# A two-block transformer layer on one core: regrouped RWKV and attention products, token and adaptive-vector work moved ahead, and a priority for one stream

## The chip, the cores and the metric

The kernel is one program on one core of a Trainium2 chip. The time is microseconds of the device, from the first to the last instruction of the execution and what lies around it. TensorE (PE in the profile) multiplies, VectorE (DVE) and ScalarE (ACT) work on tiles element by element, GpSimd (POOL) computes a few powers, and SyncE (SP) issues nearly all transfers. Matmul results go to PSUM, everything else lives in SBUF or in device memory.

## What is computed

Two blocks follow each other on a sequence of 1024 tokens of width 1024, all in float32. The first mixes tokens by sliding-window attention and by an RWKV-7 recurrence, then comes a feed-forward with a three-tap convolution; the second modulates its input by adaptive vectors made from a condition `c`, and mixes by two gated linear attentions and a stick-breaking attention.

```python
def first_block(...):
        h = rms_norm(x, norm_mix_pre[l])
        proj = h @ w_in[l]
        q, k, v, p = jnp.split(proj, (D_ATTN, D_ATTN + D_KV, D_ATTN + 2 * D_KV), axis=-1)
        attn = sliding_window_sink_attention(q, k, v, rel_bias, sinks[l])
        ...
        rw = rwkv7_time_mix(p, ...)
        mix = jnp.concatenate([attn, rw.astype(x.dtype)], axis=-1) @ w_out[l]
        x = x + rms_norm(mix, norm_mix_post[l])
        f = conv_gated_ffn(rms_norm(x, norm_ffn_pre[l]), w_ffn_up[l], conv_w[l], conv_b[l], w_ffn_down[l])
        x = x + rms_norm(f, norm_ffn_post[l])

def second_block(...):
        ada = c_act @ w_ada[l] + b_ada[l]
        shift, scale, gate = jnp.split(ada, 3, axis=-1)
        h = rms_norm_2(x) * (1.0 + scale[:, None, :]) + shift[:, None, :]
        p = h @ w_in[l]
        ...
        y = jnp.concatenate([o_a, o_b, o_c], axis=-1) @ w_out[l]
        x = x + gate[:, None, :] * y
    return rms_norm_2(x) * final_norm_w
```

## The kernel before

**Products.** Every large product is made of three: both operands are split into a high and a low part (`hi`/`lo`, `wh`/`wl`, by `split`: ACT copies the high part, DVE subtracts it), and `gemm` (L151) adds high x low, low x high and high x high in PSUM. Weights arrive by `load_parts` (L135) in tiles of 256 KB, `wr`, three buffers deep. Inputs of a projection stand transposed, features on partitions: `to_h` (L232) transposes four 128 x 128 pieces on PE into a PSUM tile, ACT copies the high part, DVE makes the low part. Small products (RWKV, attention, gated linear attention) are plain float32; a float32 matmul leaves two records in the trace.

**Tokens.** They go in two halves of 512. Each half is projected (`proj1`), mixed, put through `w_out` (`out_rows`, L743 to L745), normalised (`post_mix`) and transposed into the feed-forward's input `h`.

**Streams.** Work is written as Python generators. `weave` takes the next step of the stream whose own clock is furthest behind, where each step yields a cost and a stream has a rate; a stream can also give its instructions a priority (`ahead`, which becomes `tc.high_priority(offset=...)`). A scheduler then puts the instructions of each engine in one fixed order, by these priorities and by its own estimate of when operands are ready. An engine runs its own list in order, so one that waits holds all behind it. Memory is by pools: a tile of a pool that is opened later can lie where tiles of a closed pool lay, and waits until they are free.

There are four such weaves around the change:

1. projection of both halves, `rwkv_a`, `rwkv_b`, `rwkv_c` of the first four pieces of 128 tokens, with attention beside (`attend`);
2. `enter` (the first half's `out_rows`, `post_mix` and `to_h`, two row tiles at a time) with the rest of attention, and `rest` (RWKV of the last four pieces) beside. Its priority is `AM`, and there is none. Behind it attention's pools are closed and the feed-forward's pool `fp` is opened in the room that they leave;
3. the feed-forward of both halves (`ffn`, units of `w_up` and `w_down`), with `between`: after the last RWKV piece (`("c", 7)`) it does the second half's `out_rows`, `post_mix` and `to_h`, then `ada_vectors`, then the second block's first projection;
4. `fill`, the second block's projections (`units`, in the order `ORD`) and `out_rows`, beside `gated` (gated linear attention) and `sticks` (stick-breaking).

**`rwkv_c`.** For each piece of 128 tokens and each chunk `c` of 64, with `j` over four pairs of heads and `h` over the two heads of a pair: L594 multiplies the running state `St` (rows 0 to 63 or 64 to 127, by head) into `ou[h][0:64, 1]`, DVE adds that to `UV`; L601 makes the state's increment; L606 (state) and L608 (inside the chunk) add up in `ou[h][.., 0]`, one right behind the other for each `j` and `h`. `ou[0]` and `ou[1]` are two banks of PSUM.

**Attention.** Blocks of 128 queries. Scores are made for four groups `w`, one PSUM buffer of the two of pool `psa` each (L664), DVE adds the bias and takes the maximum (L668), ACT takes the exponent, PE transposes (L686) into the same two buffers, ACT copies, PE multiplies by the values (L698) into a buffer that is held to the block's end, and L720 transposes the result.

**`ada_vectors`.** Three vectors of 1024. For each, eight row blocks of `w_ada` are loaded (512 KB, two buffers `wa`) and added up on DVE with the weight `sc[:, k]` into `m`; a product with ones sums over partitions (L950, in PSUM pool `psx`), the bias is added, and a row is written to device memory.

**`proj2(1)`.** After the last unit of the first half, it loads the second block's tokens 4 to 7, normalises (`pre2`), transposes each, and only then begins with units of the second half. `hi` and `lo` have one buffer, so the new input is written when the old one has been read for the last time.

```python
            for i in range(4):
                xs = new_xs()
                pre2(4 + i, xs, *w)
                to_h(xs, i, hi, lo)
                yield 3
```

## Time and profile before

| what | value |
|---|---|
| time, median of 3 runs | 2600.23 us (2585.8 to 2609.15) |
| time of the profiled execution | 2600.69 us |
| its span, first to last instruction | 2598.9 us |
| mean granted TensorE clock | 0.968 |
| busy share of PE, weight loads, DVE, ACT, POOL | 95%, 75%, 65%, 45%, 4% |
| DMA | 320.78 MB, mean 123 GB/s |

Busy times of engines are sums over the span. A row of a group gives line, engine, operation, tiles and shapes, count, busy time, mean of one, and the idle time of the engine ahead of it with what ended most of it. A row in order of time gives start, duration, engine, line, operation, tiles, shapes and how many instructions were merged, and in brackets the idle time ahead and what ended it. A row of a stretch gives its bounds, its length, busy time and instructions of PE, weight loads (PEld), DVE, ACT and POOL, the granted TensorE clock as a share of full speed, the share of DMA engines busy, and GB/s. Matmuls overlap, so the step from one start to the next is the price of one, not its duration.

### The profile page before, as it was taken

The numbers are of one execution on the slowest core, as the hardware profiler recorded it, in microseconds if no ns is written. First come the engines' busy times: TensorE is split into PE (matmuls) and PEld (weight loads), VectorE is DVE, ScalarE is ACT, GpSimd is POOL, SyncE is SP. The second block draws the span as 40 slices with busy tenths as digits, with TensorE's granted clock in tenths as the row PEclk, the third lists the DMA queues.
The fourth block names the chain that finished last, engine by engine and source line by source line (L and its number), as shares of the span: only waits on it lengthen the run. The fifth ranks groups of instructions, "written<-read, shape, count | busy, mean of one in ns | idle before, by whom it ended". The sixth has DMA issues, their size and how long they took to land.

```text
span 2598.9 us, 40965 instructions
## 1 busy us (share of the span) xinstructions
PE 2480.5 (95%) x15310; PEld 1940.4 (75%) x15310; DVE 1695.4 (65%) x3676; ACT 1171.0 (45%) x2205; POOL 99.4 (4%) x138
## 2 busy tenths in 40 slices
PE   7999999899999999999988999999999989999987
PEld 5777777678787787878776888778887766777665
DVE  5466653664675674755687655545567897878887
ACT  4344332463433533334443333443345665566864
POOL 1001000000000000000000000000000000000000
PEclk9999998889999999999999999999999989999988
DMA  6433223542232332324486432243346425342437
GB/s 205 145 111 102 69 77 100 159 128 81 86 97 72 94 94 69 96 70 130 136 278 199 130 98 94 83 130 121 94 139 208 132 97 159 123 129 77 143 132 251
DMA packets 219998, 320.78 MB, mean 123 GB/s; under 512 B 56956, under 2 KB 95508, under 8 KB 219799
## 3 DMA queue, kind: packets, MB, share of 16 engines
q1 hardware_dynamic: 219798, 318.17, 38.9%
q8 instruction: 120, 1.97, 0.3%
q14 instruction: 80, 0.65, 0.1%
HBM read 270.88 MB, written 47.21 MB: 122 GB/s over the span
## 4 chain that ended last, share of the span: by engine, by line
PE 73%; DVE 10%; issue 6%; DMA 4%; ACT 4%; POOL 2%; SPq 0%; POOLq 0%; DVEq 0%; ACTq 0%
PE g L151 37%; PE d L151 11%; PE gr L743 2%; DVE wl L78 1%; PE gr L744 1%; PE gr L745 1%; DMA wa<-in_w_ada_dram 1%; PE ou L608 1%; PE ou L606 1%; PE R L1463 1%; PE ra L495 1%; PE s L1359 1%; PE a_ps L698 1%; DMA wr<-in_w_out_dram 1%; PE x L743 1%
## 5 line engine op out<-in xcount | busy, mean ns | idle before, releaser
L75 ACT ACTIVATE wh<-wr 128x512 fp32r<-128x512 f32 x712 | 443.7, 626 | 664.3 <-PE g L151 223.2
L151 PE MATMUL g<-hi,wl 128*128 128x512 f32 (+1 forms) x1680 | 678.0, 404 | 7.9 <-DVE wl L78 3.4
L151 PE MATMUL g<-hi,wh 128*128 128x512 f32 (+1 forms) x1680 | 668.9, 398 | 0.0
L151 PE MATMUL g<-lo,wh 128*128 128x512 f32 (+1 forms) x1680 | 667.6, 397 | 0.0
L78 DVE TENSOR_TENSOR wl<-wr,wh 128x512 fp32r<-128x512 f32 x712 | 484.4, 684 | 224.9 <-ACT wh L75 223.1
L151 PEld LDWEIGHTS g<-hi,wl 128*128 128x128 f32 (+1 forms) x1680 | 317.6, 189 | 86.3 <-issue 6.3
L151 PEld LDWEIGHTS g<-hi,wh 128*128 128x128 f32 (+1 forms) x1680 | 317.5, 189 | 72.5 <-issue 3.1
L151 PEld LDWEIGHTS g<-lo,wh 128*128 128x128 f32 (+1 forms) x1680 | 317.8, 189 | 71.6 <-issue 5.1
L81 DVE SCALAR_TENSOR_TENSOR cv<-g,CW,cv 128x511 f32<-128x511 f32 (+1 forms) x256 | 190.5, 744 | 186.0 <-ACT cv L75 185.8
L151 PE MATMUL d<-hh,wl 128*128 128x512 f32 x512 | 204.1, 403 | 7.1 <-DVE wl L78 2.2
L151 PE MATMUL d<-hl,wh 128*128 128x512 f32 x512 | 202.8, 396 | 0.1
L151 PE MATMUL d<-hh,wh 128*128 128x512 f32 x512 | 201.9, 395 | 0.0
L75 ACT ACTIVATE cv<-g,CW 128x512 f32<-128x512 f32 x128 | 99.5, 777 | 195.3 <-PE g L151 195.1
L78 DVE TENSOR_TENSOR acc<-d,acc 128x512 f32<-128x512 f32 x112 | 76.5, 688 | 83.4 <-PE d L151 83.3
L151 PEld LDWEIGHTS d<-hh,wl 128*128 128x128 f32 x512 | 96.9, 190 | 34.3 <-DVE acc L78 4.4
L151 PEld LDWEIGHTS d<-hl,wh 128*128 128x128 f32 x512 | 97.2, 190 | 22.5 <-DVE hl L78 2.8
L151 PEld LDWEIGHTS d<-hh,wh 128*128 128x128 f32 x512 | 97.1, 190 | 20.2
L743 PE MATMUL gr<-wl,hi 128*128 128x512 f32 x200 | 84.7, 424 | 6.3 <-DVE wl L78 4.6
L744 PE MATMUL gr<-wh,lo 128*128 128x512 f32 x200 | 81.0, 405 | 1.7 <-DVE lo L78 1.7
L745 PE MATMUL gr<-wh,hi 128*128 128x512 f32 x200 | 80.4, 402 | 0.0
L125 POOL TENSOR_TENSOR rs<-ms,half_c 128x1 f32<-128x1 f32 x48 | 31.1, 650 | 1129.4 <-DVE ms L85 1118.7
L75 ACT ACTIVATE hh<-cv 128x512 fp32r<-128x512 f32 x64 | 40.4, 631 | 70.1 <-DVE cv L78 69.7
(484 smaller groups left out, 3634.0 us busy)
## 6 DMA issues: line engine op xcount, KB each, us to landing
wr<-in_w_up_dram SPq DMA_DIRECT2D x256, 256.0 KB, 2.7
wr<-in_w_in_dram SPq DMA_DIRECT2D x160, 256.0 KB, 2.8
wr<-in_w_down_dram SPq DMA_DIRECT2D x128, 256.0 KB, 2.7
wr<-in_w_out_dram SPq DMA_DIRECT2D x100, 256.0 KB, 2.9
wr<-in_w_values_dram SPq DMA_DIRECT2D x64, 256.0 KB, 2.8
xt<-x SPq DMA_DIRECT2D x24, 512.0 KB, 4.6
wa<-in_w_ada_dram SPq DMA_DIRECT2D x24, 512.0 KB, 4.7
xt<-in_x_dram SPq DMA_DIRECT2D x16, 512.0 KB, 3.7
```

What stands on the lines that cost most here:

```text
L75: S.activation(out=out, in_=in_, func=func, **kw)
L78: (eng or V).tensor_tensor(out=out, in0=in0, in1=in1, op=op)
L81: V.scalar_tensor_tensor(out=out, in0=in0, scalar=scalar, in1=in1, op0=op0, op1=op1)
L125: G.tensor_tensor(out=dst, in0=src, in1=half_c[0:src.shape[0], 0:src.shape[1]], op=ALU.pow)
L151: T.matmul(out=ps, lhsT=l, rhs=r, start=(first and n == 0), stop=(last and n == 3 * len(wk) - 1))
L495: T.matmul(out=gp[:, q, :], lhsT=flat(BK[hb:hb + 64, 4 * b + q, :, :]), rhs=flat(AR[hb:hb + 64, 4 * b + q, 0:2, :]), start=True, stop=True)
L606: T.matmul(out=ou[h][ob:ob + 64, 0, j, :], lhsT=AR[hb:hb + 64, 2 * j + c, 0, :], rhs=St[hb:hb + 64, j, :], start=True, stop=False)
L608: T.matmul(out=ou[h][ob:ob + 64, 0, j, :], lhsT=MT[:, 2 * j + c, h, 0:64], rhs=UV[:, 2 * j + c, hb:hb + 64], start=False, stop=True)
L698: T.matmul(out=pv[:, h, :], lhsT=pt[:, i, kb, :], rhs=vtok[:, n - 1 + kb, 64 * g:64 * g + 64], start=(kb == kbs[0]), stop=(kb == 1))
L743: T.matmul(out=p, lhsT=hi[:, k, tok], rhs=wl, start=first, stop=False)
L744: T.matmul(out=p, lhsT=lo[:, k, tok], rhs=wh, start=False, stop=False)
L745: T.matmul(out=p, lhsT=hi[:, k, tok], rhs=wh, start=False, stop=last)
```

## The change

Four things change, and no product is added or dropped.

In `rwkv_c`, L594's products take the heads in turn for each pair `j`, both additions to `UV` follow, all products of the state (L606) come next, then the increment, then all products inside the chunk (L608). The first of the state's products of a bank clears it, the others add.

In `attention`, two groups of scores, one for each key group (partitions 0 to 63 and 64 to 127), take both PSUM buffers at once, and their products alternate.

`ada_vectors` moves to the beginning of `between`, ahead of the wait for the last RWKV piece, with larger costs (`YA`) at each step, and its totals use PSUM pool `psd`. Tokens 4 to 7 are loaded and normalised by a new `prepare2` after 11 units of the first half (`NP2`); two of them stay in the buffers they were loaded to, and squares of these are taken in halves. `proj2(1)` then only transposes, at priority `AP2`.

`AM` goes from 0 to 300, which gives every instruction of `enter` priority.

```diff
-AA, AB, AC, AM = 250, 400, 300, 0
+AA, AB, AC, AM = 250, 400, 300, 300
+NP2, AP2 = 11, 250
+YA = 14
...
         for c in range(2):
             ob = 64 * c
+            for j in range(4):
+                for h in range(2):
+                    hb = 64 * h
+                    T.matmul(out=ou[h][0:64, 1, j, :], lhsT=AR[hb:hb + 64, 2 * j + c, 1, :], rhs=St[hb:hb + 64, j, :],
+                             start=True, stop=True)
             for h in range(2):
                 hb = 64 * h
-                for j in range(4):
-                    T.matmul(out=ou[h][0:64, 1, j, :], ...)
                 tt(UV[0:64, c:8:2, hb:hb + 64], ou[h][0:64, 1], UV[0:64, c:8:2, hb:hb + 64], ADD)
+
+            for j in range(4):
+                for h in range(2):
+                    hb = 64 * h
+                    T.matmul(out=ou[h][ob:ob + 64, 0, j, :], lhsT=AR[hb:hb + 64, 2 * j + c, 0, :], rhs=St[hb:hb + 64, j, :],
+                             start=j == 0, stop=True, skip_group_check=True)
             sp = psr_t([128, 4, 64])
...
-                    T.matmul(out=ou[h][ob:ob + 64, 0, j, :], lhsT=AR[hb:hb + 64, 2 * j + c, 0, :], rhs=St[hb:hb + 64, j, :],
-                             start=True, stop=False)
                     T.matmul(out=ou[h][ob:ob + 64, 0, j, :], lhsT=MT[:, 2 * j + c, h, 0:64], rhs=UV[:, 2 * j + c, hb:hb + 64],
-                             start=False, stop=True)
+                             start=False, stop=True, skip_group_check=True)
...
-            for w in range(4):
-                g = w % 2
-                sp = psa_t([128, 2, 256])
-                st = at.tile([128, 2, 256], F32, tag="st", name="st", bufs=4)
+            for w in (0, 2):
+                sps = [psa_t([128, 2, 256]) for _ in range(2)]
                 for i in range(2):
-                    T.matmul(out=sp[:, i, ko:], lhsT=qt[64 * g:64 * g + 64, 2 * (w // 2) + i, :],
-                             rhs=kT[64 * g:64 * g + 64, k0:k0 + nk], start=True, stop=True)
...
+                    for g in range(2):
+                        T.matmul(out=sps[g][:, i, ko:], lhsT=qt[64 * g:64 * g + 64, w + i, :],
+                                 rhs=kT[64 * g:64 * g + 64, k0:k0 + nk], start=True, stop=True)
...
     def between():
 
         nonlocal ap, shp, ps_x, evp
+        pa = ExitStack()
+        ap = pool("ap", 1, stack=pa)
+        yield from ada_vectors()
+        pa.close()
         yield from after(("c", 7))
...
-        pa = ExitStack()
-        ap = pool("ap", 1, stack=pa)
-        yield from ada_vectors()
-        pa.close()
+        yield 0.1
...
+    def prepare2():
+
+        yield from need1_x2()
+        scale1, shift = pre2_weights()
+        for i in range(4):
+            if i < 2:
+                xs = new_xs()
+                pre2(4 + i, xs, scale1, shift)
+            else:
+                xs = xt_load(x2_d[4 + i])
+                r = rstd_halves(xs)
+                stt(xs, xs, r, scale1, MUL, MUL)
+                tt(xs, xs, shift, ADD)
+            ready.append(xs)
+            yield 1.5
...
             hi, lo = new_h()
-            w = pre2_weights()
             for i in range(4):
-                xs = new_xs()
-                pre2(4 + i, xs, *w)
-                to_h(xs, i, hi, lo)
-                yield 3
+                with tc.high_priority(offset=AP2):
+                    to_h(ready.pop(0), i, hi, lo)
+                yield 1
...
-        yield from units(0, ORD[0], psg_t)
+        yield from units(0, ORD[0][:NP2], psg_t)
+        yield from prepare2()
+        yield from units(0, ORD[0][NP2:], psg_t)
         yield from proj2(1)
```

The scheduler's order shows what comes of it at three places. In the new file the lines are others: L594 becomes L601, L606 becomes L610, L608 becomes L621, L664, L686, L698 and L720 of attention become L676, L700, L712 and L734, and L151 becomes L153.

First, PE in the first weave, in `rwkv_c` of a piece, before (`ou` with its number is one of the two banks):

```order
L495 MATMUL ra<-AR,BK 128x128 x4
L664 MATMUL a_ps<-kT,qt 128x256
L606 MATMUL ou_2718<-St,AR 64x64
L608 MATMUL ou_2718<-UV,MT 64x64
L606 MATMUL ou_2719<-St,AR 64x64
L608 MATMUL ou_2719<-UV,MT 64x64
```

The same engine, place and products after:

```order
L514 MATMUL ra<-C,AR 128x128 x3
L700 MATMUL a_ps<-C,st 128x128
L610 MATMUL ou_1864<-St,AR 64x64 x4
L621 MATMUL ou_1864<-UV,MT 64x64 x4
L700 MATMUL a_ps<-C,st 128x128 x2
L610 MATMUL ou_1865<-St,AR 64x64 x4
L621 MATMUL ou_1865<-UV,MT 64x64 x4
```

Products of the state and products inside the chunk, which alternated one by one, stand in groups of four.

Second, PE in the second weave, before: `gr` with `mh` and `ml` is `out_rows` of the first half, `a_ps` is attention.

```order
L720 MATMUL a_ps<-C,ao 128x128
L664 MATMUL a_ps<-kT,qt 128x256 x2
L720 MATMUL a_ps<-C,ao 128x128 x3
L745 MATMUL gr<-wh,mh 128x512
L743 MATMUL gr<-wl,mh 128x512
L744 MATMUL gr<-wh,ml 128x512
L664 MATMUL a_ps<-kT,qt 128x256 x4
```

After, at the same blocks of attention; `g` is the last of 48 products of the feed-forward's first two units:

```order
L153 MATMUL g<-hi,wh 128x512
L700 MATMUL a_ps<-C,st 128x128 x4
L712 MATMUL a_ps<-vtok,pt 128x64 x8
L734 MATMUL a_ps<-C,ao 128x128 x4
L676 MATMUL a_ps<-kT,qt 128x256 x8
L700 MATMUL a_ps<-C,st 128x128 x8
L712 MATMUL a_ps<-vtok,pt 128x64 x4
```

The rows of `out_rows` that stood between attention's have gone ahead, and attention's stand by themselves, with RWKV products further down.

Third, DVE at the seam between the two halves in the fourth weave, before: `lo<-trx` is the low part of the new input, `xs<-xs,shift` the end of a token's preparation, the others belong to `sticks` and `gated`.

```order
L78 TENSOR_TENSOR lo<-trx,hi 128x4x128
L81 SCALAR_TENSOR_TENSOR se<-w,se 128x512
L78 TENSOR_TENSOR w<-w,R 128x512
L78 TENSOR_TENSOR xs<-xs,shift 128x1024
L78 TENSOR_TENSOR sl<-se,sh 128x512
L78 TENSOR_TENSOR w<-w,C_16659 128x2x128
L85 TENSOR_SCALAR ssn<-ssn 128x8
```

After, the end of the same seam:

```order
L80 TENSOR_TENSOR lo<-trx,hi 128x4x128
L80 TENSOR_TENSOR w<-w,C_16659 128x2x128
L80 TENSOR_TENSOR sl<-se,sh 128x512
L80 TENSOR_TENSOR lo<-trx,hi 128x4x128 x2
L80 TENSOR_TENSOR w<-w,R 128x512
```

The preparation of tokens no longer stands between the pieces of the new input; the first of these and the last were 51 rows apart and are 21 apart now.

## The prediction

> **What bounds the kernel now.** I read the page first (busy shares, slices, chain), then busy time by stretch, then order in time where PE idles or its clock falls. The busy shares and the chain that ended last say whose time counts:

> ```profile
> span 2598.9 us, 40965 instructions
> PE 2480.5 (95%) x15310; PEld 1940.4 (75%) x15310; DVE 1695.4 (65%) x3676; ACT 1171.0 (45%) x2205; POOL 99.4 (4%) x138
> PEclk9999998889999999999999999999999989999988
> PE 73%; DVE 10%; issue 6%; DMA 4%; ACT 4%; POOL 2%; SPq 0%; POOLq 0%; DVEq 0%; ACTq 0%
> ```

> PE (TensorE) works 2480 of 2599 us and carries 73% of the chain. So time is won in three ways only: fewer PE microseconds for the same products, fewer of the 118 us in which PE idles, fewer stretches at a lowered clock. By stretch (length; then busy PE, weight load, DVE, ACT, POOL; granted clock; DMA):

> ```profile
> 170.00:455.00 285.00, 275.49 (x2151) 213.95 (x2151) 165.88 (x535) 107.73 (x250) 18.81 (x31) 0.95 0.31 90
> 570.00:597.00 27.00, 25.82 (x158) 21.27 (x156) 12.81 (x30) 13.58 (x34) 2.02 (x3) 0.50 0.42 138
> 600.00:1170.00 570.00, 565.06 (x3217) 449.51 (x3216) 352.05 (x753) 220.64 (x370) 18.47 (x22) 0.99 0.28 84
> 1316.00:1430.00 114.00, 102.58 (x412) 78.65 (x410) 90.56 (x132) 39.88 (x69) 3.49 (x4) 0.94 0.72 238
> 1430.00:1690.00 260.00, 256.43 (x1126) 207.49 (x1125) 154.22 (x258) 99.05 (x162) 1.06 (x2) 1.00 0.31 100
> 2077.00:2146.00 69.00, 60.48 (x668) 45.33 (x668) 62.50 (x151) 47.36 (x98) 2.80 (x3) 0.85 0.29 96
> 2146.00:2275.00 129.00, 125.91 (x1130) 93.48 (x1132) 98.39 (x240) 69.10 (x136) 2.02 (x2) 1.00 0.45 141
> ```

> To be seen: the two RWKV stretches (170 to 455, 600 to 1170) are full of PE work. The weak places are 570 to 597 (busy, but at half clock), 1316 to 1430 (11.4 us idle) and 2077 to 2146 (8.5 us idle, clock 0.85).

> **Grouped RWKV products.** Per head pair and chunk, L606 (state) and L608 (inside the chunk) alternate now, two records to a product:

> ```profile
> L594 PE MATMUL ou<-St,AR x256: 218/218/366, 211.2 to 1161.2; 64*64 64x64 f32 x128
> L606 PE MATMUL ou<-St,AR x256: 218/267/366, 220.4 to 1167.5; 64*64 64x64 f32 x128
> L608 PE MATMUL ou<-UV,MT x256: 222/270/367, 220.7 to 1167.7; 128*64 128x64 f32 x128
> ...
> 217.23 1.14 PE L573 MATMUL rb__1772<-W,TT 64*64 64x64 f32 x16
> 218.30 0.55 PE L686 MATMUL a_ps<-C,st 128*128 128x128 f32 x3
> ...
> 221.17 0.68 PE L601 MATMUL ra<-UV,BKt 128*64 128x64 f32 x14
> 221.78 0.32 PE L606 MATMUL ou<-St,AR 64*64 64x64 f32 x2
> ...
> 222.41 0.32 PE L606 MATMUL ou<-St,AR 64*64 64x64 f32 x2
> 222.66 0.33 PE L608 MATMUL ou<-UV,MT 128*64 128x64 f32 x2
> 222.92 0.33 PE L606 MATMUL ou<-St,AR 64*64 64x64 f32 x2
> ...
> 225.67 0.96 PE L594 MATMUL ou<-St,AR 64*64 64x64 f32 x16
> 226.56 0.44 PE L511 MATMUL ra<-C,BK 128*128 128x128 f32 x2
> ```

> Starts tell the price: each change between L606 and L608 comes 0.255 us after the last, so the 128 + 128 products take 256 x 0.255 = 65 us. Products of one form in a row cost 0.056 us a record (L594: 0.89 over 16) to 0.067 (L573: 1.07 over 16). In the new order both kinds stand in runs, nearly all of four or eight products, 55 runs in all. 512 records x 0.0615 = 31.5 us, and a change of form adds 0.255 - 2 x 0.0615 = 0.13 us, 55 times: 7 us. Saved: 65 - 38.5 = 27 us (24 with 0.067; 33 with 0.056 and half of the changes). L594 now goes to the two halves of the array in turn. The nearest row that alternates halves is L601, 0.61 over 14 = 0.044 a record: 256 x (0.056 - 0.044) = 3 us (0 to 7). Half of these 30 us lies in the first stage, where waits of other engines already leave 9.5 of 285 us idle, and I count 0.8 of it, 12 us. The other half lies between 600 and 1170, where PE is busy 99%: 15 us. **Minus 27** (20 to 33).

> **Grouped attention scores.** The new code puts the two key groups (partition halves) side by side.

> ```profile
> 531.29 1.17 PE L664 MATMUL a_ps<-kT,qt 64*128 64x256 f32 x8
> 532.39 0.50 PE L745 MATMUL gr<-wh,mh 128*128 128x512 f32 x1
> ...
> 548.11 1.89 PE L664 MATMUL a_ps<-kT,qt 64*128 64x256 f32 x8
> 549.92 0.50 PE L745 MATMUL gr<-wh,mh 128*128 128x512 f32 x1
> ```

> Eight records took 1.10 us where halves happened to mix and 1.81 where not: 0.71 for eight. Four blocks of 16 records in the first stage are 8 x 0.71 = 5.7 us; some runs stay broken, one block is narrower: **minus 4** (0 to 6). The later four blocks belong to the next term. The pair needs both score buffers at once, so PE waits for DVE between pairs.

> **Priority for the stream that makes the feed-forward's input.** Its products (L743 to L745) now run without attention between them; attention's last three blocks follow alone, after two feed-forward units (48 products) whose evacuation waits for attention's memory.

> ```profile
> 490.25 0.40 PE L745 MATMUL gr<-wh,mh 128*128 128x512 f32 x1
> ...
> 499.84 1.97 PE L232 MATMUL trx<-C,y 128*128 128x128 f32 x8
> ...
> 512.37 0.79 PE L743 MATMUL gr<-wl,mh 128*128 128x512 f32 x1
> ...
> 565.21 0.66 PE L720 MATMUL a_ps<-C,ao 128*128 128x128 f32 x4
> 565.80 1.90 PE L664 MATMUL a_ps<-kT,qt 64*128 64x256 f32 x8
> ...
> 573.70 0.90 PE L559 MATMUL rb__5588<-TT,UV 64*64 64x64 f32 x10 [1.18 <-ACT TT L75]
> ...
> 590.31 1.12 PE L720 MATMUL a_ps<-C,ao 128*128 128x128 f32 x4
> ...
> 595.80 0.79 PE L151 MATMUL g<-hi,wl 128*128 128x512 f32 x1
> ```

> Now: first pair of rows done at 490.6, products again at 512.4, first feed-forward product at 595.8. Then, on this clock: the normalisation chain in between takes the same 9.3 us (490.6 to 499.8), the second row follows sooner, products again at about 506. 96 products at 0.228 us (from 1430 to 1690 1126 such matmuls kept PE busy for 256.4 us) are 22, and 2 more at low clock: 530. A second chain of 14 us: 544. The 48 feed-forward products, 11: 555. The end of the first block, 2.5. Three blocks: the last block before took 25.6 us (565.8 to 591.4) at half clock with transposes and RWKV products in it, the one ahead 17.8 (548.1 to 565.9) at full clock with row products in it. Alone, but most likely at half clock, I take 20 each: 617.5, and 5 for RWKV products behind. Off come the 11 us of feed-forward products and 5 of RWKV products done early: 606.5 against 595.8. **Plus 11**; the ends are 17.8 a block (plus 4) and 25.6 (plus 28).

> Why half clock: between 570 and 597 PE idled 1.2 us in all, in one gap, and the clock stood at 0.50. The stretch held narrow products only, as the lone blocks will. [...]

> **Early adaptive vectors.** 24 loads of 512 KB, 24 DVE passes and 12 matmul records go from 1310 to 1412 to the first half of the feed-forward, with totals in another pair of PSUM buffers.

> ```profile
> L939 SPq DMA_DIRECT2D wa<-in_w_ada_dram x24: 327/328/786, 1309.6 to 1400.9; - x24
> L81 DVE SCALAR_TENSOR_TENSOR adam<-wa,sc,adam x21: 1271/1283/1286, 1323.4 to 1405.8; 128x1024 f32<-128x1024 f32 x21
> ...
> 1374.27 2.42 PE L950 MATMUL x<-adam,ones 128*128 128x512 f32 x4 [2.57 <-DVE adam L81]
> ```

> Of the 11.4 us idle in 1316 to 1430, the quiet stretch behind would have 1.6 (3.6 of 260). 9.8 us go; the clock, 0.94 for 114 us, gives up to 5 more. At the new place DVE has room: 352 of 570 us, and the passes add 24 x 1.28 = 31. DMA is busy 0.28 there. The loads stand on SP between weight loads, and each waits for a pass two before it; what is queued behind is the next weight tile, for which ACT's split and then PE wait. On PE the next feed-forward product is queued behind each total, which waits for the last pass. **Minus 11** (0, if every wait moves along, to 15).

> **Early tokens.** Loading and normalising rows 4 to 7 goes ahead of the last units of the first half; only transposes, at raised priority, remain at the seam. With it go four row loads, two broadcasts, the squares, four POOL powers and eight DVE passes; SP and POOL have them earlier, behind nothing that PE needs at once. The seam lost 8.5 us idle and 0.15 x 69 = 10.4 to the clock; the stretch behind would idle 1.7: 17 us. On DVE the rows from the first to the last piece of the new input fall from 51 to 21, so 0.6 of the loss goes, 10 us. It counts only if later waits let it: x 0.8, **minus 8** (0 to 14). Two DVE sums and two ACT squares are added (two rows are squared in halves). They cost nothing while PE has its units to multiply; bare, each would be below the 1.28 us of a full row's pass, 5 us together.

> **Sum.** -27 - 4 + 11 - 11 - 8 = -39 us. The profiled execution took 2600.7, the median of the runs is 2600.2: the same. Forecast 2562 us.

> **Rivals.** [...] (2) The lone blocks cost 25.5 us each: plus 28 instead of 11, 2579. For it: no weight work is left to fill PE's in-order waits. (3) The two moves pay nothing, because the same waits show at the new places: 2562 + 19 = 2581. Against it: DVE and DMA stand far lower there. (4) Slower: on SP's queue, a load of the adaptive matrix that waits for its buffer holds the weight tile behind it, and PE idles. If each of 24 + 3 loads cost the 2.57 us of the worst row above, 27 x 2.57 = 69 us: 2562 + 11 + 69 = 2642. It makes the kernel slower by 1% from 2.0 us a load on ((2626.7 - 2573) / 27). Against it: packed five times as densely, the same loads cost 11.4 / 24 = 0.5 us each. That the grouping does not arrive is excluded by the new order.

> **How the numbers follow.** Forecast 0.55, (1) 0.10, (2) 0.14, (3) 0.13, (4) 0.08. All far ends together give 2537 and, the other way, 2609; 2535 to 2600 leaves out (4) and the worst of (2) with (3), under 0.2. One per cent, 26 us, is what a measurement here tells from no change. Faster (under 2574.7): most of the forecast, 0.52, (1), and 0.03 of the others: 0.65. Within: 0.27. Slower: (4), 0.08.

> **What would show it.** Right: L610 and L621 runs with steps near 0.06 us; 600 to 1170 shorter by some 15 us; no PE wait on the adaptive vectors over 1 us; the gap at the second seam cut to under half; a stretch of lone attention with granted clock 0.5. Wrong: steps of L621 still near 0.13; weight tiles late while adaptive loads run; the first feed-forward evacuation later than 630.

## The result and the profile after

| what | before | after |
|---|---|---|
| time, median of 18 runs each, on the same chip in turn | 2603.84 us | 2580.81 us |
| lowest and highest run | 2577.84 to 2619.22 | 2566.40 to 2591.44 |
| ratio of after to before, 95% interval | | 0.9919 (0.9896 to 0.9942) |
| profiled execution: span, mean granted clock | 2598.9 us, 0.968 | 2580.5 us, 0.960 |

The kernel became 23 us faster by the medians (21 by the ratio, 15 to 27 by its interval): 0.8%, where 39 had been forecast. Below, first the page of the changed kernel: span, busy time by engine, clock in 40 slices.

```profile
span 2580.5 us, 40937 instructions
PE 2458.0 (95%) x15310; PEld 1933.0 (75%) x15310; DVE 1692.1 (66%) x3678; ACT 1172.4 (45%) x2209; POOL 99.5 (4%) x138
PEclk9999899875999999999999999999999999999989
```

PE is busy 22 us less, with the same 15310 records, and the mean clock is lower all the same: the slices with 7 and 5 (517 to 645 us) are new. They are the second weave. The next rows are stretches of the changed kernel: from the first product of `enter` to the second row group of the feed-forward's down products, then the part of it in which attention stands alone, the second half's mixing without the adaptive vectors, and the second seam.

```profile
450.00:762.00 312.00, 282.08 (x1404) 225.14 (x1403) 173.63 (x384) 129.80 (x264) 11.84 (x18) 0.81 0.36 115
558.00:647.00 89.00, 77.97 (x489) 64.76 (x488) 36.12 (x129) 27.16 (x77) 0.73 (x5) 0.55 0.27 85
1296.00:1443.00 147.00, 142.34 (x636) 115.02 (x637) 109.79 (x188) 67.01 (x121) 8.53 (x13) 0.99 0.51 167
2053.00:2122.00 69.00, 63.25 (x737) 47.40 (x736) 59.81 (x156) 45.05 (x95) 0.00 (x0) 1.00 0.26 83
```

The rows of the kernel before that answer to the first and the third of these:

```profile
461.00:739.00 278.00, 267.77 (x1406) 210.88 (x1406) 165.83 (x380) 128.53 (x264) 11.56 (x17) 0.90 0.36 110
1281.00:1451.00 170.00, 154.45 (x647) 120.76 (x648) 140.79 (x220) 67.93 (x121) 9.98 (x14) 0.95 0.69 231
```

The same work (1404 against 1406 records) takes 312 us instead of 278: PE idles 30 us instead of 10, and the clock stands at 0.81 instead of 0.90. The other stretches of the program got shorter, but for the last: behind the second seam the changed kernel takes 459 us and the kernel before 453. How far the changed kernel stands ahead (minus) or behind, milestone by milestone of the two profiled executions:

| milestone, start of | before, us | after, us | difference |
|---|---|---|---|
| first product of `enter` | 461.5 | 449.7 | -11.8 |
| `enter`'s last product, end | 564.9 | 524.7 | -40.2 |
| feed-forward's down products, group 0 | 649.3 | 680.3 | +31.0 |
| group 7 | 1281.3 | 1295.8 | +14.5 |
| group 9 (`between` is through) | 1451.3 | 1443.1 | -8.2 |
| first unit behind the second seam | 2145.6 | 2121.4 | -24.2 |
| end of the span | 2598.9 | 2580.5 | -18.4 |

`enter` ends 40 us earlier, and what it makes the input for begins 31 us later. The PE rows between, in order of time, show why: the last row product, the chain of normalisation, two feed-forward units, and then attention (L676 to L734) with RWKV among it up to 646.75.

```profile
524.26 0.40 PE L759 MATMUL gr<-wh,mh 128*128 128x512 f32 x1
...
545.28 0.77 PE L153 MATMUL g<-hi,wl 128*128 128x512 f32 x1
...
558.03 0.39 PE L153 MATMUL g<-hi,wh 128*128 128x512 f32 x1
...
562.65 0.66 PE L734 MATMUL a_ps<-C,ao 128*128 128x128 f32 x4 [1.92 <-DVE ao L80]
563.24 2.83 PE L676 MATMUL a_ps<-kT,qt 64*128 64x256 f32 x8
...
582.89 0.66 PE L734 MATMUL a_ps<-C,ao 128*128 128x128 f32 x4 [0.79 <-DVE ao L80]
...
605.92 1.11 PE L734 MATMUL a_ps<-C,ao 128*128 128x128 f32 x4
...
634.59 1.11 PE L734 MATMUL a_ps<-C,ao 128*128 128x128 f32 x4
...
646.75 0.77 PE L153 MATMUL g<-hi,wl 128*128 128x512 f32 x1
```

From 558.4 to 646.8, 88 us, there is no wide product (128 x 512) on PE; the longest such stretch before was 31 us.

### The profile page after: what moved, and what is told of

The parts are those of the page before. It is cut to its first block, busy times and chain, and to the rows that moved or that the text cites. A ratio compares the mean times of both kernels' runs of the same rounds, so it can differ in the third digit from the quotient of the medians.

```text
span 2580.5 us, 40937 instructions
## 1 busy us (share of the span) xinstructions
PE 2458.0 (95%) x15310; PEld 1933.0 (75%) x15310; DVE 1692.1 (66%) x3678; ACT 1172.4 (45%) x2209; POOL 99.5 (4%) x138
## 3 DMA queue, kind: packets, MB, share of 16 engines
q8 instruction: 120, 1.97, 0.3%
## 4 chain that ended last, share of the span: by engine, by line
PE 62%; DVE 9%; ACT 2%; DMA 2%; issue 2%; POOL 1%; SPq 0%; POOLq 0%; ACTq 0%; DVEq 0%
PE g L153 32%; PE d L153 11%; DVE wl L80 1%; PE gr L757 1%; PE s L1400 1%; PE gr L758 1%; PE R L1504 1%; PE gr L759 1%; PE x L757 1%; PE x L759 1%; PE x L758 1%; PE a_ps L712 1%; PE z L1489 1%; DVE tmp L80 1%; PE po L1522 1%
## 5 line engine op out<-in xcount | busy, mean ns | idle before, releaser
L153 PE MATMUL g<-hi,wl 128*128 128x512 f32 (+1 forms) x1680 | 676.1, 402 | 6.7 <-ACT ev L77 1.8
L153 PE MATMUL g<-hi,wh 128*128 128x512 f32 (+1 forms) x1680 | 668.5, 398 | 0.0
L153 PE MATMUL g<-lo,wh 128*128 128x512 f32 (+1 forms) x1680 | 667.2, 397 | 0.0
L153 PEld LDWEIGHTS g<-hi,wl 128*128 128x128 f32 (+1 forms) x1680 | 317.2, 189 | 82.7 <-issue 3.5
L153 PEld LDWEIGHTS g<-hi,wh 128*128 128x128 f32 (+1 forms) x1680 | 317.0, 189 | 71.5 <-issue 2.9
L153 PEld LDWEIGHTS g<-lo,wh 128*128 128x128 f32 (+1 forms) x1680 | 317.2, 189 | 71.1 <-issue 5.0
L153 PE MATMUL d<-hh,wl 128*128 128x512 f32 x512 | 201.8, 398 | 4.9 <-DVE acc L80 1.6
L153 PE MATMUL d<-hl,wh 128*128 128x512 f32 x512 | 201.3, 393 | 0.2 <-DVE hl L80 0.2
L153 PE MATMUL d<-hh,wh 128*128 128x512 f32 x512 | 200.3, 392 | 0.0
L153 PEld LDWEIGHTS d<-hh,wl 128*128 128x128 f32 x512 | 95.5, 188 | 32.9 <-ACT hh L77 5.3
L153 PEld LDWEIGHTS d<-hl,wh 128*128 128x128 f32 x512 | 96.2, 188 | 22.5 <-DVE hl L80 3.6
L153 PEld LDWEIGHTS d<-hh,wh 128*128 128x128 f32 x512 | 96.2, 188 | 19.7
```

The costliest lines, as they stand in the source:

```text
L153: T.matmul(out=ps, lhsT=l, rhs=r, start=(first and n == 0), stop=(last and n == 3 * len(wk) - 1))
```

## The experiments

Theory A: the priority of `enter` alone lost some 40 us, because it took the rows' products away from beside attention. Rival B: it cost the 11 us of the prediction, and other parts paid less. All ratios are to the kernel before, which ran in turn on the same chip (2603 to 2607 us). Each profiled execution is split below as well: length of a piece of the program, PE's idle time in it, and the time lost to the clock (length at half clock times 0.5, an estimate: 148 narrow records that took 22.8 us at half clock took 12.8 us in another execution, as the last section shows).

### The parts one by one

The changed kernel without the priority:

```diff
-AA, AB, AC, AM = 250, 400, 300, 300
+AA, AB, AC, AM = 250, 400, 300, 0
```

> The changed kernel with AM = 0: all parts but the priority of `enter`. Theory A (the priority alone lost about 40 us, because it left three attention blocks without wide products beside them): some 40 us below the changed kernel's 2581, 2535 to 2548, ratio to the kernel before 0.974 to 0.979, and no stretch of PE without wide products longer than the 31 us of the kernel before. Rival B (the priority cost the 11 us of the prediction, and other parts paid less than predicted): 2566 to 2574, ratio 0.987.

Measured: 2532.99 us (2524.76 to 2541.18), ratio 0.974 (0.9705 to 0.9775). That is 48 us below the changed kernel (47 by the ratios). The stretch from `enter` to the second row group:

```profile
435.00:702.00 267.00, 252.55 (x1406) 201.24 (x1406) 172.61 (x384) 128.07 (x262) 11.01 (x18) 0.93 0.44 134
```

The stretch takes 267 us instead of 312, for the same work, at clock 0.93, and the longest piece without wide products is 23 us. Theory A holds, though the time is 2 us below the range it gave, and rival B falls.

The priority alone, in the kernel before:

```diff
-AA, AB, AC, AM = 250, 400, 300, 0
+AA, AB, AC, AM = 250, 400, 300, 300
```

> The kernel before with AM = 300 and nothing else. Theory A: 30 to 45 us slower, ratio 1.012 to 1.017, with a stretch of over 80 us on PE without wide products, at granted clock 0.5 for most of it. Rival B: 11 us slower, ratio 1.004. If the loss needs the other parts (the shorter first stage, the early adaptive vectors on DVE), it is near 1.000.

Measured: 2640.21 us, ratio 1.015 (1.0104 to 1.0196), 39 us slower (27 to 51). Its rows, the whole stretch and the part with attention alone:

```profile
452.00:767.00 315.00, 288.48 (x1408) 228.49 (x1406) 165.42 (x377) 130.31 (x265) 11.34 (x17) 0.82 0.32 96
558.00:652.00 94.00, 84.80 (x516) 68.87 (x514) 29.37 (x120) 27.34 (x78) 0.73 (x5) 0.55 0.13 36
```

The same picture without any of the other parts: the loss needs only the priority.

The grouped RWKV products alone (the kernel before with the new body of the chunk loop in `rwkv_c`):

```diff
...
+            for j in range(4):
+                for h in range(2):
+                    T.matmul(out=ou[h][ob:ob + 64, 0, j, :], lhsT=AR[..., 0, :], ..., start=j == 0, stop=True, ...)
...
-                    T.matmul(out=ou[h][ob:ob + 64, 0, j, :], lhsT=AR[..., 0, :], ..., start=True, stop=False)
                     T.matmul(out=ou[h][ob:ob + 64, 0, j, :], lhsT=MT[...], rhs=UV[...], start=False, stop=True, ...)
```

> The kernel before with the grouped RWKV products alone. The prediction's term: 27 us faster (20 to 33), ratio 0.990 (0.987 to 0.992). From the milestones of the two traces: 11 us by the end of the first stage and 16 in the first half of the feed-forward, 27 as well. Rival: the waits of the first stage give its part back, 15 us faster, ratio 0.994.

Measured: 2561.73 us, ratio 0.9852 (0.9819 to 0.9885), 38 us faster (30 to 47). Added up from start to next start over the three lines' 768 records, their products took 83.4 us before and 48.7 now: 35 us, and the time fell by about as much. The waits of the first stage gave nothing back.

The adaptive vectors alone (`ada_vectors` at the beginning of `between`, `total` in PSUM pool `psd`, costs `YA`):

```diff
+        pa = ExitStack()
+        ap = pool("ap", 1, stack=pa)
+        yield from ada_vectors()
+        pa.close()
         yield from after(("c", 7))
```

> The kernel before with the adaptive vectors moved ahead and nothing else. The prediction's term: 11 us faster (0 to 15), ratio 0.996. From the milestones of the two traces the stretch between 1281 and 1451 got 22 us shorter: if all of that is the move, ratio 0.991. Rival: the loads and passes among the feed-forward delay weight tiles there, and the kernel is not faster, ratio 1.000 or more.

Measured: 2589.57 us, ratio 0.9949 (0.9923 to 0.9974), 13 us faster (7 to 20). At their old place:

```profile
1287.00:1435.00 148.00, 142.74 (x635) 114.89 (x636) 110.20 (x189) 67.28 (x121) 8.52 (x13) 0.99 0.52 166
```

So 170 us become 148, all 22 us of it by this move. But group 7 of the down products starts 6 us later (1287.3 against 1281.3), of which 1 us was there at group 0 and 5 come in the first half of the feed-forward, where the passes and products now are (in the changed kernel the 12 records of the totals alone are 6.6 us there, as shown further down), and about 1 more is given back behind the seam (16.1 ahead at group 15, 14.8 at the end). What PE waits for most between 600 and 1300 is RWKV, 3.5 us in three pieces (3.4 in the kernel before); it waits for weights 1.0 us. So the rival, weight tiles that come late, falls.

The early tokens alone (`prepare2`, `proj2(1)` with transposes only, `fill` cut at `NP2`), and the paired scores alone (the new score loop of `attention`):

```diff
-        yield from units(0, ORD[0], psg_t)
+        yield from units(0, ORD[0][:NP2], psg_t)
+        yield from prepare2()
+        yield from units(0, ORD[0][NP2:], psg_t)
```

> The kernel before with the early tokens (early preparation, priority only for the transposes at the seam) and nothing else. The prediction's term: 8 us faster (0 to 14), ratio 0.997. From the traces of before and after the seam itself is 17 us shorter and 6 come back later, 11 us, ratio 0.996. Rival: the units that follow had waited for weights there anyway, and nothing is left, ratio 1.000.

Measured: 2591.39 us, ratio 0.9956 (0.9926 to 0.9986), 11 us faster (4 to 19).

```diff
-            for w in range(4):
-                g = w % 2
-                sp = psa_t([128, 2, 256])
+            for w in (0, 2):
+                sps = [psa_t([128, 2, 256]) for _ in range(2)]
```

> The kernel before with the paired attention scores and nothing else. The prediction's term: 4 us faster (0 to 6), ratio 0.998. Rival: since the changed kernel without priority begins `enter` 10 us earlier than the kernel with grouped RWKV products alone, the pairing is worth about 10 us, ratio 0.996. Other rival: PE waits for DVE between two pairs, since both score buffers are taken at once, and nothing is won, ratio 1.000 or more.

Measured: 2596.54 us, ratio 0.9956 (0.9933 to 0.9979), 11 us faster (6 to 17). The 128 records of the score products, from start to next start, take 26.0 us instead of 30.4, 4.4 less. Where the rest of the 11 comes from, if it isn't the measurement, stays open.

### What it is about the priority that costs

The same priority, but on the normalisation and the transposes of `enter` alone, none on its products:

```diff
+                with tc.high_priority(offset=300):
                     post_mix(i + j, yt, *pw)
...
+                with tc.high_priority(offset=300):
                     to_h(yt, i + j, *h)
```

> The changed kernel with AM = 0, but with the same priority (300) on `post_mix` and `to_h` of `enter` alone, and none on its products. Theory A (the loss comes from taking the rows' products away from beside attention): within 10 us of the kernel with AM = 0, 2523 to 2543, and no stretch without wide products over 40 us. Rival C (the loss comes from putting the normalisation ahead of attention's own DVE and ACT work): 2560 to 2580, as the changed kernel.

Measured: 2536.63 us, ratio 0.9722 (0.9688 to 0.9755), the same as without priority. Its longest piece without wide products is 25 us, so rival C falls: it is the products of the rows, drawn together, that leave attention bare. Hurrying the chain costs nothing that these runs can tell, and brings nothing.

Smaller priorities put the rows' products together only in part. From the first product of `enter` to the second row group of the down products, in the profiled executions:

| AM | median, us | ratio (95%) | stretch, us | idle PE | lost to the clock | longest piece without wide products |
|---|---|---|---|---|---|---|
| 0 | 2532.99 | 0.974 (0.9705 to 0.9775) | 267.3 | 14.4 | 18.8 | 23.4 us, 184 records |
| 30 | 2550.43 | 0.977 (0.9719 to 0.9821) | 278.2 | 18.9 | 23.9 | 32.4, 142 |
| 60 | 2548.19 | 0.9772 (0.9727 to 0.9817) | 278.5 | 24.2 | 18.8 | 25.4, 104 |
| 120 | 2567.16 | 0.9837 (0.9791 to 0.9883) | 298.9 | 26.5 | 42.7 | 66.8, 402 |
| 300 | 2580.81 | 0.9919 (0.9896 to 0.9942) | 312.7 | 30.0 | 58.0 | 88.3, 484 |

> The changed kernel with AM = 30. In the order of its PE instructions, narrow products from the rows' products on stand in groups of 33, 96 and 59 between wide ones (46 and 107 with AM = 0). Theory A (time follows the longest stretches without wide products, because the clock falls there): no slower than with AM = 0, 2523 to 2540. Rival E (any priority of the rows' products costs, in proportion to how early they stand): halfway to the changed kernel, 2550 or more.

> The changed kernel with AM = 60: groups of 29, 72 and 84 narrow products between wide ones. Theory A: as with AM = 0 or 30, 2523 to 2545. Rival E: 2550 to 2570.

> The changed kernel with AM = 120: groups of 30, 53 and then 228 narrow products. Theory A: one long stretch of about half the changed kernel's 484 records, so about half of its loss, 2550 to 2565, the clock at 0.5 through most of that stretch. Rival E: nearly the whole loss, 2570 to 2580.

With 60 the clock loses no more than without priority, and still the stretch is 11 us longer, 10 of them idle; with 30 it is 11 us longer too, 5 by the clock and 4.5 idle. That PE then waits for the normalisation with less work beside it is the likely reason, not tested by itself. The medians are 15 to 17 us above AM = 0: above theory A's ranges in both runs, just inside rival E's with 30 and just under it with 60. By the ratios the difference is 8 us and the intervals overlap, so these two runs don't decide between the theories. With 120 the median lies between the two ranges; there is one piece of 66.8 us, and its row shows the half clock:

```profile
562.00:628.00 66.00, 58.95 (x395) 49.92 (x395) 24.74 (x92) 23.09 (x63) 0.73 (x5) 0.56 0.25 70
```

Theory A was too simple in one point, then: the idle time of PE counts beside the clock. Between AM = 0 and 300 the stretch grows by 45.4 us: 39.2 lost to the clock, 15.6 of waits, less 9.4 in the rest, part of which is that waits overlap half clock.

### Is it the clock, and is it the width?

That a stretch has half clock does not show that the clock is what costs, nor that narrow products bring it down. So wide products that only occupy PE were put into the last three attention blocks of the changed kernel, ahead of the first use of each PSUM tile (what they write is overwritten):

```diff
+        def cover(ps):
+            if n >= 5:
+                for _ in range(2):
+                    T.matmul(out=flat2(ps), lhsT=wide[0][:, 0:128], rhs=wide[0], start=True, stop=True)
...
             pv = psa_t([128, 8, 64])
+            cover(pv)
```

> The changed kernel (AM = 300) with two added products of 128 x 128 by 128 x 512 ahead of the first use of each PSUM tile of the last three attention blocks, ten places a block; what they write is overwritten, so they only occupy PE, 20 x 0.23 = 4.6 us a block at full clock, 13.8 us together. Theory A1 (the clock falls because only narrow products stand there): the granted clock of the three blocks goes from 0.55 to 0.9 or more, they get shorter by 20 to 30 us less 14, so the time is 0 to 20 us below that of the changed kernel. Rival D (the clock falls because of the waits between attention's steps, or the half clock is no matter of the products): the clock stays at 0.5, the added products cost 28 us at half clock, and the time is 2600 to 2610.

Measured: 2590.75 us, ratio 0.994 (0.9915 to 0.9966). Neither theory's numbers came: the clock rose, but to 0.77 instead of 0.9, and the time did not fall. The rows of the stretch, and of the part from 579 to 618, where the clock stood at full:

```profile
552.00:647.00 95.00, 84.34 (x521) 62.31 (x520) 40.42 (x151) 30.00 (x80) 0.73 (x5) 0.77 0.25 72
579.00:618.00 39.00, 34.36 (x239) 22.82 (x237) 18.22 (x88) 14.47 (x45) 0.73 (x5) 1.00 0.12 29
```

The half clock begins at 560.9 and again at 618.9, and in each case the 3.4 us ahead (3.41 is the shortest piece of half clock in the traces of before and after) held no wide product, while two to four in each 3.4 us had kept it up for nearly 40 us. In that part PE was no busier than in the lone stretch of the changed kernel: 34.36 of 39 us against 77.97 of 89, 88% in both, at clock 1.00 and 0.55. So it isn't the idle share of PE that sets the clock here. Two at each place were too few to cover the whole stretch. With five:

```diff
-                for _ in range(2):
+                for _ in range(5):
```

> As the kernel with two added products at each place, but with five, 50 a block, so that nearly every 3.4 us of the three last attention blocks holds five or more products of 128 x 512. Theory A1 (the clock falls in a stretch of 3.4 us that follows one with hardly any wide product): granted clock 0.95 or more from the second lone block to the end of the last, where the kernel with two had 0.77; the added work, 3 x 50 x 0.23 = 34 us, is paid partly by the clock, so the time is 2590 to 2605. Rival D (the clock falls because of the waits between attention's steps): it still falls to 0.5 for more than 20 us there, and the time is over 2610.

Measured: 2580.64 us, ratio 0.9915 (0.9896 to 0.9935). The whole stretch, the part with attention alone, and that part up to its last half clock and from there on:

```profile
450.00:760.00 310.00, 282.34 (x1559) 223.84 (x1558) 174.11 (x385) 131.13 (x265) 11.87 (x18) 0.94 0.39 117
558.00:647.00 89.00, 81.71 (x526) 66.41 (x527) 39.68 (x146) 32.26 (x84) 0.73 (x5) 0.94 0.26 74
558.00:628.00 70.00, 64.08 (x422) 51.64 (x422) 31.38 (x131) 23.98 (x71) 0.73 (x5) 1.00 0.27 78
628.00:639.00 11.00, 9.63 (x69) 8.17 (x69) 4.84 (x9) 5.37 (x8) 0.00 (x0) 0.53 0.17 50
```

150 products were added, 34 us of work at 0.23 each, and the time is the same within the intervals (ratios 0.9915 and 0.9919): the clock goes from 0.55 to 0.94 and pays for them. It stood at 1.00 to 628, beyond the end of the last lone block (625.0); the half clock behind it falls where 9 us hold RWKV products and no wide one. The clock came out as theory A1 forecast, and the time 10 us below its range of 2590 to 2605: the clock paid not for part of the added work but for all of it. Rival D falls. This settles the first question and most of the second: the clock there follows from the lack of wide products, not from the waits, and its price in the changed kernel was about the 34 us of work that now fit in beside (41 by the time lost to the clock, 58.0 and 17.1). What in the wide products does it is not shown: they are of another type too (`F32R`, the narrow ones plain float32), so that width and type were not told apart. It is no way to win the time, since the cover must be work that is needed anyway; AM = 0 is that.

AM = 0 is also the best kernel found (with the priority on the normalisation alone it is the same within the intervals), 2.6% below the kernel before.

## Why the prediction came out as it did

The time is 19 us above the forecast of 2562 and inside its range of 2535 to 2600, and the chance of 0.27 for "within 1%" is what happened. But the forecast was near by luck, because errors cancel: the priority cost far more than its term, and the other parts paid more than theirs. Its terms, and each part measured alone (with the intervals; sums are of unrounded ratios):

| term | predicted | measured alone |
|---|---|---|
| grouped RWKV products | -27 (-20 to -33) | -38 (-30 to -47) |
| paired scores | -4 (0 to -6) | -11 (-6 to -17); -4.4 in their own products |
| priority | +11 (+4 to +28) | +39 (+27 to +51); +47 beside the other parts |
| adaptive vectors | -11 (0 to -15) | -13 (-7 to -20) |
| tokens | -8 (0 to -14) | -11 (-4 to -19) |
| sum | -39 | -36; -21 (-15 to -27) together, and -68 without the priority, where the single ones give -75 |

**The step that failed: the size of the priority's term.** It was put at 11 us with 28 as its far end, and measured 39 alone and 47 beside the other parts. The mechanism was right (lone attention at half clock, between 558 and 647), and so was the price taken for a block, 20 us: from 563.2 to 635.7 the three blocks took 72.5 us, of which about 15 are RWKV products between them, so 19 each. What the sum left out stands around the blocks. On the clock of the kernel before (10.9 us are added to the times after, since the first pair of rows ended so much earlier), the first feed-forward product behind attention was put at 622.5 and came at 657.7:

- the two waits for normalisation and the rows between: products of the second pair at 509 (506 forecast), the feed-forward's input at 556 (544), the 48 products done at 569 (555): 14 us. Without attention's products beside it, PE sat through the chain: three rows below show 5.00, 3.96 and 2.05 us of it, where the longest wait of PE in the kernel before, from 461 to 739, is 1.5;
- "5 for RWKV products behind": the RWKV products drawn into the stretch, 15 between the blocks and 11 behind them, took 26 us at half clock. That is 21 us more, and by the start of down group 0 only about 4 have come back as work done early;
- the end of the first block took 5.0 instead of 2.5, and three blocks 58 instead of 60: nothing together.

14 + 21 - 4 = 31 on top of the predicted 11: 42, the step from -11 to +31 in the milestones. PE in the changed kernel, where the waits are:

```profile
486.45 1.22 PE L502 MATMUL ra<-AR,BK 64*128 64x128 f32 x4 [5.00 <-DVE ms L87]
...
494.88 1.94 PE L247 MATMUL trx<-C,y 128*128 128x128 f32 x8 [3.96 <-DVE y L83]
...
533.26 1.11 PE L247 MATMUL trx<-C,y 128*128 128x128 f32 x4 [2.05 <-DVE y L83]
```

The prediction's rival (2) gave 2579, near the time, by 25.6 us a block. The blocks did not cost that; it was near for another reason. Rival (1), with its chance of 0.10, stood for full clock in the lone blocks, plus 4. No run shows that for blocks left bare: the clock there was 0.55 in the changed kernel and 0.55 with the priority alone. Nor did a long wait of PE go with the half clock: between 583.7 and 648.5 it stood at 0.50 throughout, and the longest wait of PE in it was 1.9 us.

**Grouped RWKV products: right, but too small.** The steps came as forecast:

```profile
216.95 0.96 PE L610 MATMUL ou<-St,AR 64*64 64x64 f32 x16
217.84 0.69 PE L616 MATMUL ra<-UV,BKt 128*64 128x64 f32 x16
218.36 1.10 PE L621 MATMUL ou<-UV,MT 128*64 128x64 f32 x16
219.39 0.33 PE L514 MATMUL ra<-C,AR 128*128 128x128 f32 x1
```

0.89 / 16 = 0.056 for the state, 1.03 / 16 = 0.064 inside the chunk. In the experiment the three lines gave 35 us where 30 had been counted. L606 and L608 took 68.0 us before (65 counted) and 36.6 after (38.5 counted), in 61 runs instead of 55; with the 0.0615 us a record of the forecast that leaves about 0.08 us for a change of form, not 0.13; L594 gave 3.4 (3 counted). The factor of 0.8 for the first stage, which stood for the waits, had no ground: in the experiment, 16 us of the gain are there by the first product of `enter`, 19 more between down groups 0 and 7 (forecast 12 and 15).

**Adaptive vectors: right in sum, by other terms.** The old place gave 22 us, not the 15 of its far end. The stretch also lost the 24 passes from DVE (141 to 110 us busy), which the term left out; that they made the difference is not shown. The new place costs 5, where nothing was put down for PE: the 12 records of the totals came along, and there they are on the path. PE in the changed kernel, between products of the feed-forward:

```profile
771.99 0.40 PE L153 MATMUL d<-hh,wh 128*128 128x512 f32 x1
772.23 2.07 PE L957 MATMUL d<-adam,ones 128*128 128x512 f32 x4
774.44 0.50 PE L153 MATMUL d<-hh,wl 128*128 128x512 f32 x1
```

Four of them take 2.2 us from start to next start, three times that is 6.6. No wait of PE ahead of the totals exceeds 0.8 us, and the longest for a weight tile between 600 and 1300 is 1.0, as in the kernel before. So rival (4) fell.

**Early tokens: right in sum, by other terms.** In the changed kernel the lead grows from 6.5 to 24.2 us at the seam and is 18.4 at the end. So nearly all of the 17 us counted as lost there went, where 0.6 of it was forecast, and 6 were given back, where 2 were. The sign named for it did not come: PE's idle time there is 5.8 us against 8.5, not half. What went is the half clock, 0.85 to 1.00.

**Scores: in part.** The term counted the four blocks of the first stage, whose score records took 2.8 us less (13.2 and 10.4), inside its range; why the part alone gives 11 is open.

Of the signs that were to show the prediction right, only the idle time at the second seam failed. Of those that were to show it wrong, one came: the first evacuation of the feed-forward's products (`cv<-g` on ACT) is at 639, later than 630. It named the right place.

## What to carry to other kernels

Here narrow products among wide ones mostly ran at full clock (0.95 from 170 to 455 us of the kernel before), and alone at half (0.50 for 64.9 us in the changed kernel). So before a stream of wide products is moved ahead, count what it has been covering: not only the blocks that are named, but all that a scheduler will draw into the gap. A stream that finishes 40 us earlier, as `enter` did, is worth nothing if what it feeds waits for something else. Test each part of a change alone: here one part took back two thirds of what the others had won.

## What was not expected of the hardware

| a window with | at full clock: next one half | at half clock: next one half |
|---|---|---|
| none | 26 of 75 | 110 of 118 |
| 1 to 4 | 20 of 173 | 27 of 37 |
| 5 or more | 1 of 1488 | 2 of 31 |

One to four mostly kept the state that stood, full (153 of 173) or half (27 of 37). No window without work was needed for half clock: in the 36 windows from 533 to 656 us of the kernel with two added products, 14 of them at half clock, PE idled at most 1.6 of the 3.4 us.

**The same products in the same order, in 22.8 us and in 12.8.** The first 2742 records on PE, to 425.7 and 416.1 us, are the same ones in the same order in the changed kernel and with AM = 0. One run of 148 narrow records took 22.8 us (255.8 to 278.6, at a granted clock of 0.50) in the one execution and 12.8 (258.0 to 270.8) in the other. Clock and work between 240 and 290, first the changed kernel, then AM = 0:

```profile
240.00:290.00 50.00, 49.41 (x370) 38.99 (x369) 20.57 (x53) 13.48 (x35) 2.48 (x6) 0.66 0.28 81
```

```profile
240.00:290.00 50.00, 49.01 (x469) 39.45 (x470) 29.97 (x74) 20.55 (x52) 6.18 (x9) 0.97 0.34 91
```

Of the nine kernels with the grouped RWKV products, seven had the long form in their profiled execution, among them kernels with AM = 0, 30, 120 and 300, and the two short ones have 0 and 60, so it doesn't go by the priority. About 10 of the 57 us between these two profiled spans lie in this one run, likely by chance, and medians of many runs are to be compared: they are 48 apart. The spread of one kernel's runs goes with the clock: over 18 runs of the changed kernel, from 2566.40 us at a mean clock of 0.968 to 2591.44 at 0.957, time and clock are correlated by -0.91.
